# Moving the GpSimd arithmetic of a hybrid mixer to VectorE and ScalarE

## The chip, the core and the metric

The kernel runs on one core of a Trainium2 chip. A core has five engines with their own instruction streams: TensorE (PE, matrix products; PEld is its weight load), VectorE (DVE), ScalarE (ACT), GpSimd (POOL) and SyncE (SP). Here SP and POOL also issue transfers between HBM and the on-chip memory SBUF. Each engine works through its stream strictly in order and waits on semaphores that other engines raise. The metric is device time in microseconds of one launch; lower is better.

## The reference

Two layers (DEPTH 2) of a decoder trunk on 512 tokens with model width 1024, all float32. What matters here is the mixer in the middle of each layer:

```
h += 1/2 * SwiGLU_1(rmsnorm(h))                 # width 2816
u  = rmsnorm(h) @ w_in                          # one projection, split into three groups
  A: RG-LRU, width 256:  y = gelu(gate) * scan(a, sqrt(1 - a*a) * (i * x)),  a = exp(-8 * r * softplus(-lam))
                         r, i = sigmoid(block-diagonal products of conv(x))
  B: sliding-window attention, 8 query heads, window 128, a learned sink per head
  C: gated DeltaNet, 4 heads, chunks of 64:  T = (I + strict(beta k k' * decay))^-1,
                         u = T (beta v),  w = T (beta k exp(g));  a scan over 8 chunk states
                         o = rmsnorm(o) * dn_norm * silu(z)
h += concat(A, B, C) @ w_out
h += 1/2 * SwiGLU_2(rmsnorm(h))
h += sigmoid(rmsnorm(h) @ w_ple_gate) * (p[l] @ w_ple_proj)
```

A final RMSNorm follows the second layer.

## The kernel before

Every product that needs float32 accuracy is made of three passes of a reduced format: `split` and `weight` (L116 to L125) write a high half `wh` (a copy on ACT, L123) and a low half `wl` (weight minus high half, L124), and `mm3` (L147 to L149) multiplies high by high, high by low activations, and low by high. A weight block of the mixer's input projection has 128 x 1024 elements, and there are 15 of them (`proj(i)`, L912).

A layer runs FFN 1, the mixer, FFN 2 and the per-layer embedding one after the other. The two FFNs take most of the run and are not touched. The mixer of layer 0 lies at about 380 to 575 us of the profiled span, that of layer 1 some 1007 us later.

In the mixer the three groups are interwoven. `masked(t)` (L1262) writes, for each of four token tiles, the triangle times the log decay of each head (`tg`, high and low half), from which PE sums cumulative decays (R, L1274). `chunk(t)` (L1269) builds the decay matrices DT on DVE (L1290), the products of keys (`pk`, L1281) and the scaled queries and keys (L1297, L1306, L1309). The inverse of the 64 x 64 triangles starts with a chain of 15 steps on 16-row blocks that DVE alone does (L1364 to L1366: shuffle, multiply `row`, add to `x`); its result is laid out as TMA and TT (L1371, L1376), and PE then doubles the block size in `level` (L1386, `pinv`). The LRU is `lru_gates` (L957: products `pr` and `pi`, then sigmoid and two tanh on ACT, L968 on DVE), `lru_scan` (L970) and `lru_gelu` (L988). Attention computes scores `sc` (L1007), a maximum on DVE (L1011), exponentials on ACT (L1023) and scales the weights `e` of four heads by 1/dn (L140 on DVE or POOL, L134 on ACT). The chunk scan, its decay matrix `ei` (L1446) and the output product follow.

PE's order is written out by hand: ORDER and GAPS name the pieces and the amount of projection work that `fill` puts between them. The orders of DVE, ACT and POOL in the mixer come from the tile scheduler, which ranks ready instructions by its own cost estimate. The table OPT gives the engine of some operations: `es` the four heads of a scaling, `wlo` the low halves of projections 6 to 14, `g2` and `sx` one multiply each of the LRU. V is VectorE, A ScalarE, G GpSimd. POOL also issues the 86 accumulating weight transfers of the FFNs (L414) and multiplies at the end (L1646).

Of the kernel before, what the change touches and what calls it, by code (L numbers as in the profile page):

```python
# [9 lines left out]
F32 = mybir.dt.float32  # L10
# [29 lines left out]

OPT = {'pta': 'V', 'ptb': 'A', 'es': 'VAAG', 'uw': 'A', 'pn': 'A', 'bt': 'VA', 'sx': 'V', 'g2': 'G', 'wlo': 'GGVGVGVGG'}

# [20 lines left out]
def trunk(ctx: ExitStack, tc: tile.TileContext, a):  # L63
# [51 lines left out]

    def weight(src, k, n, via=None, raw=None):  # L116
        if raw is None:
            raw = wrp.tile([128, k, n], F32, tag="wr", name="wr")
            nc.sync.dma_start(out=raw, in_=src)
        hi = whp.tile([128, k, n], F32R, tag="wh", name="wh")  # L120
        lo = whp.tile([128, k, n], F32R, tag="wl", name="wl")
        with tc.high_priority():
            A.activation(out=hi, in_=raw, func=AF.Copy)  # L123
            (via or V).tensor_tensor(out=lo, in0=raw, in1=hi.bitcast(F32), op=ALU.subtract)  # L124
        return hi, lo  # L125
# [6 lines left out]
    def copy(eng, out, in_, scale=1.0):  # L132
        if eng == "A":
            A.activation(out=out, in_=in_, func=AF.Copy, scale=scale)  # L134
        else:
# [3 lines left out]
            else:  # L139
                e.tensor_scalar(out=out, in0=in_, scalar1=scale, scalar2=None, op0=ALU.mult)  # L140

    def eng(c):
        return V if c == "V" else G

# [734 lines left out]
    def mixer(l, norm, gain, ahead):  # L879
        xh, xl = norm.xh, norm.xl  # L880
        pl = par[:, l, :]
        with ExitStack() as es:
# [29 lines left out]
            def proj(i):  # L912
                wh, wl = weight(a["wi"][l, i], KD, 128, via=eng(OPT['wlo'][i - 6]) if i > 5 else None)
                ps = bank([128, S], "pp")
                for k in range(KD):
                    mm3(ps, wh[:, k, :], wl[:, k, :], xh[k], xl[k], k == 0, k == KD - 1)
                    yield 0.64
                return ps
# [51 lines left out]
            def lru_scan():  # L970
# [4 lines left out]
                for i in range(2):  # L975

                    r1, t_, x = lr[i], ltm[i], xr[i]
                    A.activation(out=r1, in_=r1, func=AF.Copy, scale=0.5, bias=0.5)
                    V.scalar_tensor_tensor(out=t_, in0=t_, scalar=1.0, in1=r1, op0=ALU.add, op1=ALU.mult)
                    V.scalar_tensor_tensor(out=r1, in0=t_, scalar=2.0, in1=r1, op0=ALU.subtract, op1=ALU.mult)  # L980
                    A.activation(out=t_, in_=r1, func=AF.Copy, scale=-2.0, bias=-1.0)
                    V.scalar_tensor_tensor(out=x, in0=r1, scalar=-1.0, in1=x, op0=ALU.mult, op1=ALU.mult)
                    eng(OPT['sx']).tensor_tensor(out=x, in0=sq[:, i, :], in1=x, op=ALU.mult)
                    V.tensor_tensor_scan(out=r1, data0=t_, data1=x, initial=0.0, op0=ALU.mult, op1=ALU.add)
                    lo_[i] = r1

            def lru_gelu(i, gl):
                g2 = pair("g2", i)  # L988
                A.activation(out=g2, in_=gl, func=AF.Square)
                A.activation(out=g2, in_=g2, func=AF.Copy, scale=0.044715, bias=1.0)  # L990
                eng(OPT['g2']).tensor_tensor(out=g2, in0=g2, in1=gl, op=ALU.mult)
                A.activation(out=g2, in_=g2, func=AF.Tanh, scale=0.7978845608028654)
# [238 lines left out]
            for t in range(NT):  # L1231
# [5 lines left out]
                z3 = zz[t].rearrange("p (h e) -> p h e", h=4)  # L1237
                G.tensor_tensor(out=z3, in0=z3, in1=dnn.unsqueeze(1).to_broadcast([128, 4, 64]), op=ALU.mult)

# [22 lines left out]
            def masked(t):  # L1262
                tg[t] = [dp.tile([128, 4, 128], F32R, tag="d", name="tg") for x in range(2)]
                for o, x in zip(tg[t], (gh, gl_)):
                    G.tensor_tensor(out=o, in0=tri.unsqueeze(1).to_broadcast([128, 4, 128]),
                                    in1=x.bitcast(F32)[:, 4 * t:4 * t + 4].unsqueeze(2).to_broadcast([128, 4, 128]),
                                    op=ALU.mult)

            def chunk(t):  # L1269
# [23 lines left out]
                for hh in range(2):  # L1293
                    rs = slice(64 * hh, 64 * hh + 64)
                    A.activation(out=er[rs].rearrange("p (c i) -> p c i", c=2), in_=R[rs, 2 * hh:2 * hh + 2, :],
                                 func=AF.Exp)
                G.tensor_tensor(out=qg[t], in0=kq[:, :, 1, tsl], in1=er.rearrange("p (c i) -> p c i", c=2),  # L1297
                                op=ALU.mult)
                for hh, pk in enumerate(pks):
# [5 lines left out]
                kv = ktm[t].rearrange("p c (h d) -> p h c d", h=2)  # L1305
                G.tensor_tensor(out=vk[t][:, :, 64:128].rearrange("p (h c) d -> p h c d", h=2), in0=kv,  # L1306
                                in1=eg[:, 4 * t:4 * t + 4].rearrange("p (h c) -> p h c", h=2).unsqueeze(3)
                                .to_broadcast([128, 2, 2, 64]), op=ALU.mult)
                G.tensor_tensor(out=kd[t].rearrange("p c (h d) -> p h c d", h=2), in0=kv,  # L1309
                                in1=cd[:, 4 * t:4 * t + 4].rearrange("p (h c) -> p h c", h=2).unsqueeze(3)  # L1310
# [49 lines left out]
            x16 = small("x16", 256).rearrange("p (u j) -> p u j", u=16)  # L1360
            G.tensor_copy(out=x16, in_=cst[:, K_D16:K_D16 + 16].unsqueeze(1).to_broadcast([128, 16, 16]))
            for i in range(15, 0, -1):
# [77 lines left out]
            def steps(t):  # L1440
# [3 lines left out]
                for hh in range(2):  # L1444
                    rs = slice(64 * hh, 64 * hh + 64)
                    G.tensor_tensor(out=ei[rs], in0=ident[rs, rs].unsqueeze(1).unsqueeze(1).to_broadcast([64, 2, 2, 64]),  # L1446
                                    in1=egl[rs, :, 4 * t + 2 * hh:4 * t + 2 * hh + 2].unsqueeze(3).to_broadcast([64, 2, 2, 64]), op=ALU.mult)
# [371 lines left out]
```

## Time and profile before

| what | value |
|---|---|
| median of 3 runs | 2054.86 us (2052.04 to 2055.87) |
| the profiled execution | 2052.92 us |
| its span, first to last instruction | 2051.1 us |
| PE busy | 1967.7 us (96%), granted clock 0.980 |
| DVE busy | 1509.4 us (74%) |
| ACT busy | 1002.0 us (49%) |
| POOL busy | 181.2 us (9%) |

Busy shares are means over the whole run. The change lies in two mixers, so the stretches of a mixer are what has to be read, and in them PE's waits and the state of DVE and ACT.

### The profile page before, as it was taken

Reading aid. Unit: us, or ns where it says so; the run is one execution under the profiler, and the core shown is the slowest. Engines: PE = TensorE matmul, PEld = TensorE weight load, DVE = VectorE, ACT = ScalarE, POOL = GpSimd, SP = SyncE. Lnnn points to the kernel's source line nnn. Section 1 sums busy time; section 2 is a strip of 40 time slices with the busy share of each in tenths; the row PEclk is TensorE's granted clock in tenths of the full one; section 3 lists DMA queues with packets and bytes.
Section 4 is the critical chain, followed back from the end, with each engine's and each line's share of the span. In section 5 each row is a group of like instructions: output and inputs, shape, how many; then the busy total and the mean of one; then the engine's idle time right before and its main releaser. Section 6 shows DMA issues by size and latency. Waiting matters only on the chain.

```text
span 2051.1 us, 32033 instructions
## 1 busy us (share of the span) xinstructions
PE 1967.7 (96%) x12625; PEld 1752.2 (85%) x12625; DVE 1509.4 (74%) x2620; ACT 1002.0 (49%) x1651; POOL 181.2 (9%) x197
## 2 busy tenths in 40 slices
PE   7999999999999999999989999999899999999996
PEld 5988998887778989997879899988677899899885
DVE  7875883879878856865888568647897887488466
ACT  5642652454745534643556336434366565156343
POOL 0100000042201000000000000000421000000001
PEclk8999999999999999999999999999999999999998
DMA  6763743221046745643457357322111377275411
GB/s 193 194 172 95 188 129 113 78 73 47 17 124 171 188 120 147 174 126 103 124 136 189 114 148 186 124 83 96 53 42 44 117 201 192 76 188 139 136 62 62
DMA packets 85415, 254.51 MB, mean 124 GB/s; under 512 B 9616, under 2 KB 17040, under 8 KB 85008
## 3 DMA queue, kind: packets, MB, share of 16 engines
q1 hardware_dynamic: 72880, 207.36, 31.8%
q0 software_dynamic: 12384, 45.09, 12.5%
q8 instruction: 99, 1.62, 0.3%
q14 instruction: 52, 0.43, 0.1%
HBM read 250.32 MB, written 2.10 MB: 123 GB/s over the span
## 4 chain that ended last, share of the span: by engine, by line
PE 75%; DVE 16%; ACT 4%; issue 3%; DMA 1%; SPq 0%; DVEq 0%; ACTq 0%
PE pu L475 10%; PE pg L475 10%; PE pd L147 8%; PE pd L149 8%; PE qu L475 8%; PE pd L148 8%; PE qg L475 7%; PE pp L147 2%; PE pp L148 1%; PE pp L149 1%; PE ppg L149 1%; PE ppg L148 1%; PE ppg L147 1%; DVE wl L124 1%; DVE gl L443 1%
## 5 line engine op out<-in xcount | busy, mean ns | idle before, releaser
L475 PE MATMUL pu<-T,gh 128*128 128x256 f32 x880 | 159.5, 280 | 0.0
L475 PE MATMUL pg<-T,gh 128*128 128x256 f32 x784 | 144.4, 282 | 9.5 <-ACT T L251 7.5
L443 DVE TENSOR_TENSOR gl<-wr,gh 128x1024 fp32r<-128x1024 f32 x102 | 124.6, 1221 | 26.6 <-ACT gh L438 26.6
L123 ACT ACTIVATE wh<-wr 128x1024 fp32r<-128x1024 f32 (+2 forms) x76 | 77.2, 1015 | 135.1 <-PE pp L148 50.5
L475 PEld LDWEIGHTS pu<-T,gh 128*128 128x128 f32 x880 | 134.7, 188 | 0.0
L129 DVE TENSOR_TENSOR gl<-wr,gh 128x1024 fp32r<-128x1024 f32 x53 | 64.5, 1223 | 93.6 <-ACT gh L128 93.4
L475 PEld LDWEIGHTS pg<-T,gh 128*128 128x128 f32 x784 | 121.2, 189 | 11.1 <-ACT T L251 8.1
L147 PE MATMUL pd<-X,gh 128*128 128x512 f32 x328 | 128.8, 393 | 0.0
L149 PE MATMUL pd<-X,gl 128*128 128x512 f32 x328 | 128.7, 392 | 0.0
L148 PE MATMUL pd<-X,gh 128*128 128x512 f32 x328 | 127.8, 390 | 0.0
L475 PE MATMUL pu<-T,gl 128*128 128x256 f32 x440 | 123.0, 279 | 0.0
L438 ACT ACTIVATE gh<-wr 128x1024 fp32r<-128x1024 f32 x102 | 105.2, 1046 | 19.9 <-PE pd L148 14.0
L128 ACT ACTIVATE gh<-wr 128x1024 fp32r<-128x1024 f32 x53 | 55.8, 1059 | 120.7 <-PE pd L148 95.2
L475 PE MATMUL pg<-T,gl 128*128 128x256 f32 x392 | 110.1, 281 | 0.0
L475 PE MATMUL pg<-T,wh 128*128 128x256 f32 x592 | 107.3, 280 | 2.3 <-DVE cg L554 2.3
L124 DVE TENSOR_TENSOR wl<-wr,wh 128x1024 fp32r<-128x1024 f32 (+2 forms) x64 | 74.1, 1157 | 40.9 <-ACT wh L123 40.2
L147 PE MATMUL pp<-X,wh 128*128 128x512 f32 x240 | 102.1, 425 | 0.0
L438 ACT ACTIVATE sh<-r 128x512 fp32r<-128x512 f32 x80 | 50.6, 632 | 103.6 <-DVE r L455 103.6
L149 PE MATMUL pp<-X,wl 128*128 128x512 f32 x240 | 98.2, 409 | 2.0 <-DVE wl L124 2.0
L443 DVE TENSOR_TENSOR wl<-wr,wh 128x1024 fp32r<-128x1024 f32 x67 | 81.8, 1221 | 23.4 <-ACT wh L438 23.4
L148 PE MATMUL pp<-X,wh 128*128 128x512 f32 x240 | 98.2, 409 | 0.2 <-DVE X L252 0.2
L475 PEld LDWEIGHTS pg<-T,wh 128*128 128x128 f32 x592 | 90.5, 188 | 3.2 <-DVE cg L554 2.9
(477 smaller groups left out, 6048.9 us busy)
## 6 DMA issues: line engine op xcount, KB each, us to landing
wr<-in_d_dram SPq DMA_DIRECT2D x64, 512.0 KB, 3.9
wr<-in_g_dram SPq DMA_DIRECT2D x45, 512.0 KB, 4.3
wr<-in_u_dram SPq DMA_DIRECT2D x45, 512.0 KB, 4.3
r<-in_g_dram SPq DMA_DIRECT2D x43, 512.0 KB, 3.7
r<-in_u_dram SPq DMA_DIRECT2D x43, 512.0 KB, 4.1
r<-in_g_dram POOLq DMA_DIRECT2D x43, 512.0 KB, 7.3
r<-in_u_dram POOLq DMA_DIRECT2D x43, 512.0 KB, 6.9
wr<-in_wi_dram SPq DMA_DIRECT2D x30, 512.0 KB, 3.3
```

Source lines behind the costliest of these rows:

```text
L123: A.activation(out=hi, in_=raw, func=AF.Copy)
L124: (via or V).tensor_tensor(out=lo, in0=raw, in1=hi.bitcast(F32), op=ALU.subtract)
L128: A.activation(out=hi, in_=x, func=AF.Copy)
L129: V.tensor_tensor(out=lo, in0=x, in1=hi.bitcast(F32), op=ALU.subtract)
L147: T.matmul(out=out, lhsT=wh, rhs=xh, start=start, stop=False)
L148: T.matmul(out=out, lhsT=wh, rhs=xl, start=False, stop=False)
L149: T.matmul(out=out, lhsT=wl, rhs=xh, start=False, stop=stop)
L438: A.activation(out=self.g[n][0], in_=self.of(n)[0], func=AF.Copy)
L443: V.tensor_tensor(out=g[1], in0=raw, in1=g[0].bitcast(F32), op=ALU.subtract)
L475: T.matmul(out=ps, lhsT=l_[:, q, :], rhs=r_, start=start and q == 0 and i == 0, stop=stop and q == 3 and i == 2, skip_group_check=more)
```

## The change

All tensor operations of the mixer that POOL did move. Per layer, DVE takes six low halves of projection weights (wlo), L1238 (4 instructions), L1297, L1306 and L1309 (4 each), L1446 (8 of 64 x 256) and L991 (2); ACT takes `masked` (8 instructions of 128 x 512 become 32 of 128 x 128, one per head, because ACT scales by one number per partition), the fourth head of each attention scaling (8) and the constant copy into x16 (1). POOL keeps L414 and L1646. Lines of the new kernel from L142 on have numbers lower by 3, from L1265 on by 4.

```diff
-OPT = {'pta': 'V', 'ptb': 'A', 'es': 'VAAG', 'uw': 'A', 'pn': 'A', 'bt': 'VA', 'sx': 'V', 'g2': 'G', 'wlo': 'GGVGVGVGG'}
+OPT = {'pta': 'V', 'ptb': 'A', 'es': 'VAAA', 'uw': 'A', 'pn': 'A', 'bt': 'VA'}
...
-    def weight(src, k, n, via=None, raw=None):
+    def weight(src, k, n, raw=None):
...
-            (via or V).tensor_tensor(out=lo, in0=raw, in1=hi.bitcast(F32), op=ALU.subtract)
+            V.tensor_tensor(out=lo, in0=raw, in1=hi.bitcast(F32), op=ALU.subtract)
...
-                wh, wl = weight(a["wi"][l, i], KD, 128, via=eng(OPT['wlo'][i - 6]) if i > 5 else None)
+                wh, wl = weight(a["wi"][l, i], KD, 128)
...
-                eng(OPT['g2']).tensor_tensor(out=g2, in0=g2, in1=gl, op=ALU.mult)
+                V.tensor_tensor(out=g2, in0=g2, in1=gl, op=ALU.mult)
...
-                G.tensor_tensor(out=z3, in0=z3, in1=dnn.unsqueeze(1).to_broadcast([128, 4, 64]), op=ALU.mult)
+                V.tensor_tensor(out=z3, in0=z3, in1=dnn.unsqueeze(1).to_broadcast([128, 4, 64]), op=ALU.mult)
...
-                    G.tensor_tensor(out=o, in0=tri.unsqueeze(1).to_broadcast([128, 4, 128]),
-                                    in1=x.bitcast(F32)[:, 4 * t:4 * t + 4].unsqueeze(2).to_broadcast([128, 4, 128]),
-                                    op=ALU.mult)
+                    for h in range(4):
+                        A.activation(out=o[:, h, :], in_=tri, func=AF.Copy, scale=x.bitcast(F32)[:, 4 * t + h:4 * t + h + 1])
...
-                G.tensor_tensor(out=qg[t], in0=kq[:, :, 1, tsl], in1=er.rearrange("p (c i) -> p c i", c=2),
+                V.tensor_tensor(out=qg[t], in0=kq[:, :, 1, tsl], in1=er.rearrange("p (c i) -> p c i", c=2),
...
-            G.tensor_copy(out=x16, in_=cst[:, K_D16:K_D16 + 16].unsqueeze(1).to_broadcast([128, 16, 16]))
+            A.activation(func=AF.Copy, out=x16, in_=cst[:, K_D16:K_D16 + 16].unsqueeze(1).to_broadcast([128, 16, 16]))
...
-                    G.tensor_tensor(out=ei[rs], in0=ident[rs, rs].unsqueeze(1).unsqueeze(1).to_broadcast([64, 2, 2, 64]),
+                    V.tensor_tensor(out=ei[rs], in0=ident[rs, rs].unsqueeze(1).unsqueeze(1).to_broadcast([64, 2, 2, 64]),
```

The two instructions of L1306 and L1309 change from G to V in the same way. PE's and SP's orders stay as they were. The orders of DVE and ACT in the mixer come out anew.

First place: DVE in layer 0 where the first projection behind the chunks needs its low half. LTA and DT belong to the chunks, `l` is the input of the 16-row chain. Before:

```order
L1300 TENSOR_TENSOR LTA<-pk,DT 128x256 x2
L1063 SCALAR_TENSOR_TENSOR T_4550<-pp,rb 128x512
L1302 TENSOR_TENSOR DT<-pk,DT 128x256 x2
L1354 STREAM_TRANSPOSE l_4751<-LTA 32x512 x3
L124 TENSOR_TENSOR wl<-wr,wh 128x1024
L1354 STREAM_TRANSPOSE l_4751<-LTA 32x512
L1343 TENSOR_TENSOR vk<-pv,vr 128x4x64 x2
L1357 TENSOR_SCALAR er<-l_4751,cst 128x256
```

After:

```order
L1296 TENSOR_TENSOR LTA<-pk,DT 128x256 x3
L1060 SCALAR_TENSOR_TENSOR T_4574<-pp,rb 128x512
L1296 TENSOR_TENSOR LTA<-pk,DT 128x256
L124 TENSOR_TENSOR wl<-wr,wh 128x1024
L1298 TENSOR_TENSOR DT<-pk,DT 128x256 x4
L1350 STREAM_TRANSPOSE l_4775<-LTA 32x512 x4
```

The low half (L124) stood behind three of the four transposes (L1354, now L1350) and now stands ahead of all of them, and two of the chunk's own products come behind it.

Second place: ACT in layer 0 behind the LRU's gate products (`pr`, `pi` the products, T the sigmoids, `tm` and `sq` the two tanh; a table load stands where the function set changes). Before:

```order
L965 ACT_TABLE_LOAD
L965 ACTIVATE T_4708<-pr,par 128x512
L966 ACTIVATE sq<-pi,nb 128x512
L967 ACTIVATE tm<-T_4708,lrr 128x512
L965 ACTIVATE T_4719<-pr,par 128x512
L974 ACT_TABLE_LOAD
L974 ACTIVATE T_4708<-T_4708,lsp_4287 128x512
L966 ACTIVATE sq<-pi,nb 128x512
L967 ACTIVATE tm<-T_4719,lrr 128x512
L978 ACTIVATE T_4708<-T_4708 128x512
L974 ACTIVATE T_4719<-T_4719,lsp_4287 128x512
L978 ACTIVATE T_4719<-T_4719 128x512
```

After:

```order
L962 ACT_TABLE_LOAD
L962 ACTIVATE T_4732<-pr,par 128x512
L964 ACTIVATE tm<-T_4732,lrr 128x512
L963 ACTIVATE sq<-pi,nb 128x512
L971 ACT_TABLE_LOAD
L971 ACTIVATE T_4732<-T_4732,lsp_4287 128x512
L962 ACT_TABLE_LOAD
L962 ACTIVATE T_4743<-pr,par 128x512
L963 ACTIVATE sq<-pi,nb 128x512
L975 ACTIVATE T_4732<-T_4732 128x512
L964 ACTIVATE tm<-T_4743,lrr 128x512
L969 ACT_TABLE_LOAD
```

The first sigmoid is now followed by an exponential before the second sigmoid, which puts two more table loads into the sequence, and the second `sq` comes behind both.

Third place: DVE in layer 1 where the inverse's 16-row chain (`row`, `x`) ends and TMA is laid out. Before, around TMA:

```order
L1365 TENSOR_TENSOR row<-row,x_14848 128x16
L1366 TENSOR_TENSOR x_14848<-x_14848,row 128x16
L1371 TENSOR_TENSOR TMA<-x_14848,cst 128x512 x2
L968 SCALAR_TENSOR_TENSOR T_14788<-sq,T_14788 128x512
L1371 TENSOR_TENSOR TMA<-x_14848,cst 128x512 x2
L1376 STREAM_TRANSPOSE TT<-TMA 128x512 x4
L979 SCALAR_TENSOR_TENSOR tm<-tm,T_14797 128x512
L979 SCALAR_TENSOR_TENSOR tm<-tm,T_14808 128x512
L1058 TENSOR_TENSOR T_14958<-pp,rb 128x512
L980 SCALAR_TENSOR_TENSOR T_14797<-tm,T_14797 128x512
L980 SCALAR_TENSOR_TENSOR T_14808<-tm,T_14808 128x512
L982 SCALAR_TENSOR_TENSOR T_14641<-T_14797,T_14641 128x512
```

After, ahead of TMA:

```order
L977 SCALAR_TENSOR_TENSOR T_14845<-tm,T_14845 128x512
L1362 TENSOR_TENSOR x_14896<-x_14896,row 128x16x2
L977 SCALAR_TENSOR_TENSOR T_14856<-tm,T_14856 128x512
L979 SCALAR_TENSOR_TENSOR T_14689<-T_14845,T_14689 128x512
L1361 TENSOR_TENSOR row<-row,x_14896 128x16
L1442 TENSOR_TENSOR row<-cst,egl 64x256 x2
L979 SCALAR_TENSOR_TENSOR T_14836<-T_14856,T_14836 128x512
L980 TENSOR_TENSOR T_14689<-sq,T_14689 128x512
L1362 TENSOR_TENSOR x_14896<-x_14896,row 128x16
L980 TENSOR_TENSOR T_14836<-sq,T_14836 128x512
L981 SCALAR_TENSOR_TENSOR T_14845<-tm,T_14689 128x512
L1367 TENSOR_TENSOR TMA<-x_14896,cst 128x512 x4
```

The LRU's chain of both halves up to the first scan (before: L979, L980, L982, L983, L984; now L976, L977, L979, L980, L981) stood behind TMA and TT and now stands ahead of TMA, with two of the L1446 (now L1442) among it.

## Rows read from the trace of the kernel before

**Rows 1.** POOL's groups of instructions over the whole run: busy us, mean ns; then idle before.
```profile
L124 POOL TENSOR_TENSOR wl<-wr,wh 128x1024 fp32r<-128x1024 f32 x12 | 29.3, 2443 | 146.0 <-ACT wh L123 138.3 <-PE pr L961 7.7
L140 POOL TENSOR_SCALAR e<-e,dn 128x256 f32<-128x256 f32 x12 | 11.6, 965 | 48.1 <-DVE dn L1026 33.1 <-ACT X L128 8.4 <-ACT T L134 6.7
L1446 POOL TENSOR_TENSOR row<-cst,egl 64x256 f32<-64x256 f32 x16 | 11.3, 706 | 8.7 <-DVE x L1366 4.8 <-DVE LTA L1462 3.3
L1265 POOL TENSOR_TENSOR tg<-cst,gh 128x512 fp32r<-128x512 f32 x8 | 8.3, 1040 | 6.3 <-ACT gh L128 6.3
```

**Rows 2.** Stretches of layer 0's mixer: length, each engine's busy us, granted clock, DMA share, GB/s.
```profile
440.00:480.00 40.00, 32.60 (x152) 24.03 (x151) 37.50 (x76) 14.94 (x36) 18.52 (x19) 0.94 0.17 56
...
490.00:530.00 40.00, 38.16 (x230) 32.14 (x228) 38.63 (x83) 27.29 (x48) 11.42 (x9) 0.96 0.13 44
530.00:570.00 40.00, 39.30 (x326) 27.67 (x324) 31.84 (x137) 29.00 (x97) 8.23 (x10) 1.00 0.00 1
```

**Rows 3.** PE's waits between 440 and 580 us: total us, times, longest us.
```profile
PE sc L1007 <- DVE mx L1011: 3.7, 3, 1.7
PE pk L1281 <- DVE xs L922: 3.0, 1, 3.0
PE sc L1007 <- DVE T L1099: 1.6, 1, 1.6
PE pp L149 <- DVE wl L124: 1.0, 1, 1.0
```

**Rows 4.** POOL in order of time, two of the mixer's weight halves: start, us.
```profile
453.21 2.40 POOL L124 TENSOR_TENSOR wl<-wr,wh 128x1024 fp32r<-128x1024 f32 x1
...
476.16 2.35 POOL L124 TENSOR_TENSOR wl<-wr,wh 128x1024 fp32r<-128x1024 f32 x1 [12.86 <-ACT wh L123]
```

**Rows 5.** DVE in order of time in the same stretch: start us, us taken, count at the end.
```profile
450.67 5.08 DVE L1290 SCALAR_TENSOR_TENSOR DT<-DT,b,cst 128x128 f32<-128x128 f32 x4
...
460.09 1.70 DVE L1290 SCALAR_TENSOR_TENSOR DT<-DT,b,cst 128x128 f32<-128x128 f32 x4 [0.18 <-ACT DT L1287]
...
468.57 1.23 DVE L124 TENSOR_TENSOR wl<-wr,wh 128x1024 fp32r<-128x1024 f32 x1
...
475.13 0.39 DVE L1365 TENSOR_TENSOR row<-row,x 128x224 f32<-128x224 f32 x1
...
476.63 2.11 DVE L1365 TENSOR_TENSOR row<-row,x 128x208 f32<-128x208 f32 x1
```

**Rows 6.** ACT in order of time: four small scaled copies, two per-head scalings.
```profile
443.92 1.14 ACT L1285 ACTIVATE DT<-R,gc 128x128 f32<-128x128 f32 x4
...
533.39 0.90 ACT L134 ACTIVATE e<-e,dn 128x256 f32<-128x256 f32 x2
```

**Rows 7.** Two stretches in which the granted clock was half.
```profile
478.80:485.40 6.60, 5.84 (x16) 4.56 (x17) 6.53 (x41) 2.17 (x11) 0.33 (x1) 0.51 0.18 60
523.20:526.40 3.20, 3.20 (x16) 2.79 (x14) 3.17 (x15) 2.30 (x9) 1.27 (x1) 0.52 0.36 127
```

**Rows 8.** PE in layer 1's mixer, the gate product and the inverse's first level.
```profile
1495.93 1.02 PE L961 MATMUL pr<-T,lw 128*128 128x512 f32 x2
...
1504.19 1.95 PE L1386 MATMUL pinv<-TMA,LTA 128*128 128x128 f32 x16
```

**Rows 9.** ACT in layer 1's mixer behind the gate products.
```profile
1505.11 0.63 ACT L978 ACTIVATE T<-T 128x512 f32<-128x512 f32 x1
1505.76 1.28 ACT L972 ACT_TABLE_LOAD   x1
1507.05 1.06 ACT L972 ACTIVATE sq<-tm 128x1024 f32<-128x1024 f32 x1
```

**Rows 10.** DVE in layer 1's mixer.
```profile
1502.64 2.16 DVE L1371 TENSOR_TENSOR TMA<-x,cst 128x512 f32<-128x512 f32 x2
...
1509.37 1.25 DVE L979 SCALAR_TENSOR_TENSOR tm<-tm,T 128x512 f32<-128x512 f32 x2
...
1517.59 3.15 DVE L984 TENSOR_TENSOR_SCAN T<-tm,T 128x512 f32<-128x512 f32 x2
```

More of the change, by code (lines that the diff above doesn't have):

```diff
@@ L140, in copy @@
                 e.tensor_scalar(out=out, in0=in_, scalar1=scale, scalar2=None, op0=ALU.mult)
-    def eng(c):
-        return V if c == "V" else G
     def mm3(out, wh, wl, xh, xl, start, stop):
@@ L982, in lru_scan @@
                     V.scalar_tensor_tensor(out=x, in0=r1, scalar=-1.0, in1=x, op0=ALU.mult, op1=ALU.mult)
-                    eng(OPT['sx']).tensor_tensor(out=x, in0=sq[:, i, :], in1=x, op=ALU.mult)
+                    V.tensor_tensor(out=x, in0=sq[:, i, :], in1=x, op=ALU.mult)
                     V.tensor_tensor_scan(out=r1, data0=t_, data1=x, initial=0.0, op0=ALU.mult, op1=ALU.add)
@@ L1305, in chunk @@
                 kv = ktm[t].rearrange("p c (h d) -> p h c d", h=2)
-                G.tensor_tensor(out=vk[t][:, :, 64:128].rearrange("p (h c) d -> p h c d", h=2), in0=kv,
+                V.tensor_tensor(out=vk[t][:, :, 64:128].rearrange("p (h c) d -> p h c d", h=2), in0=kv,
                                 in1=eg[:, 4 * t:4 * t + 4].rearrange("p (h c) -> p h c", h=2).unsqueeze(3)
                                 .to_broadcast([128, 2, 2, 64]), op=ALU.mult)
-                G.tensor_tensor(out=kd[t].rearrange("p c (h d) -> p h c d", h=2), in0=kv,
+                V.tensor_tensor(out=kd[t].rearrange("p c (h d) -> p h c d", h=2), in0=kv,
                                 in1=cd[:, 4 * t:4 * t + 4].rearrange("p (h c) -> p h c", h=2).unsqueeze(3)
```

## The prediction

> **What bounds the kernel now.** Read the stretches of a mixer first, then PE's waits in it, then DVE and POOL side by side, and only then the order of instructions. From 440 to 480 us DVE is busy 37.50 of 40 us while PE is busy 32.60, and from 490 to 530 DVE is at 38.63 with PE at 38.16; from 530 to 570 PE is at 39.30, and ACT is the fuller of the other two around its softmax work, with 29.00 [rows 2]. So in the first 40 us DVE sets the pace, after that PE does with DVE close behind. PE's waits say the same: all four large ones in this mixer end on DVE, 3.0 us for the key products on `xs`, 1.0 on a low half, 1.6 on T of L1099 and 3.7 in three pieces on the attention's maximum [rows 3]. They come to 9.3 us per mixer. Layer 1's mixer has the same pattern; I use layer 0's numbers for both.
>
> Part of DVE's load is not its own. Four products of L1290 took 1.70 us at 460.09, and the same four took 5.08 at 450.67, over a POOL low half that began at 453.21 and took 2.40. A `row` multiply of 208 columns took 2.11 us at 476.63, where the larger one with 224 columns just before took 0.39; POOL's low half ran from 476.16 to 478.51 and the multiply ended at 478.74 [rows 4, 5]. Both have two inputs in SBUF, and both end when POOL ends, plus their own work. The Trainium skill (SBUF — State Buffer, "SBUF: two separate sides") says that DVE and GpSimd hold one shared pair of ports as an exclusive lock for a whole instruction, also for a DVE operation with two SBUF inputs against a GpSimd operation that reads SBUF. The trace agrees: had the two shared evenly, 0.39 us would have become about 0.8, not 2.11.
>
> How much of this DVE pays per mixer lies between the 5.1 us of the two cases (3.4 and 1.7) and POOL's busy time in the three stretches, 18.52 + 11.42 + 8.23 = 38.2 us [rows 2]. I take 19, half of the upper end, since about half of what runs on DVE in these stretches has two SBUF inputs.
>
> **The change part by part.** *DVE's account.* Six low halves at 1.23 us [rows 5] are 7.4 us in place of 2.44 each on POOL [rows 1]. Sixteen instructions of 128 x 256 at 0.39, the time of the row multiply of about that size, are 6.2. Eight of 64 x 256 cost at most as much, I take 0.3: 2.4. Two of 128 x 512 at 0.62, half of the 1.25 of L979 [rows 10], are 1.2. Together 17.2 us more per mixer, against 19 less of stalls: a gain of about 2, within what I know of the 19 no gain at all. What moves the time is therefore where DVE is late, not how much it does.
>
> *The early part of a mixer.* The wait of 3.0 us on `xs` goes with the stall of 3.4 in L1290 ahead of it. Next late is the exponential `er` on ACT, which the reuse of the key products' bank needs: `masked` puts 32 copies of about 0.28 us, a quarter of 1.14 [rows 6], into ACT's queue, 9.0 us where POOL took 8 x 1.04 = 8.3 [rows 1], and some of them stand in front of `er`. I leave 1.4 of the wait: -1.6, between 0 and -3.0. The 1.0 on the low half goes, since it now stands ahead of the transposes: -1.0, at worst 0. The 1.6 on L1099 shrinks by what DVE has won by then, less the low half of 1.23 that now lies there: -0.7. Of the three waits on the maximum, the one right behind the locked multiply loses that multiply's 1.7, and gets the 1.23 of a low half: -0.5. Together -3.8 per layer, between 0 and -7.3 (3.0, 1.0, 1.6 and 1.7).
>
> *The clock.* Behind such waits the granted clock was half: 0.51 from 478.8 to 485.4, 0.52 from 523.2 to 526.4 [rows 7]. At the full level of 2.4 GHz the first stretch would have been 3.3 us shorter, the second 1.6. With shorter waits ahead I take half of each back, -1.7 and -0.8, per layer, between nothing and all.
>
> *ACT's order in layer 0.* Two more table loads at 1.28 [rows 9] stand between the gate products and the second `sq`, on which the DVE instruction ahead of TMA waits (L965 of the new kernel, L968 of the old). Counted from the first gate product, the second `sq` is ready after about 8.5 us, and that instruction and the first TMA, 0.6 each, make 9.8; PE comes to the inverse 1504.19 - 1495.93 = 8.3 us after the same product [rows 8], and layer 0 has the same distance. That is a wait of about 1.6; between 0 and 2.6 (both loads). I take +1.8 with the handover. DVE has its LRU work behind it earlier than before, and the wait of 1.7 on the maximum near 520 us goes: -1.7.
>
> *DVE's order in layer 1.* This is the large one. TMA now stands behind the whole LRU chain of both halves and the first scan, and the chain needs the second L978 on ACT. In ACT's new order that one is behind the table load and the square root. Before, it started at 1505.11; with 1.28 and 1.06 ahead of it and 0.63 of its own it ends at about 1508.0 [rows 9]. Then DVE has seven instructions of 128 x 512 at 0.62 (4.4), two of L1446 (0.6), three small steps of the 16-row chain at about 0.2 (0.6), one scan at 3.15 / 2 = 1.6, and the first TMA at 0.6: 7.8 us [rows 10], so TMA is there at 1515.8. PE comes to it at 1504.19 [rows 8]. Nothing hides that, for PE's order is fixed and every projection, score and output product is queued behind this product. PE waits 11.5 us; I see 10 as the lower end (less for each small step) and 13 as the upper one (two of the instructions took 1.4 each under POOL's stalls before). Behind it, -1.7 for the wait near 520 as in layer 0, and a stretch at half clock: by [rows 7] between 1.6 and 3.3, I take +2.5.
>
> *The tail.* The fourth head of each scaling on ACT costs 0.90 / 2 = 0.45 where POOL took 0.97 [rows 1, 6], eight times, in the stretch where ACT is at 29.00 of 40 [rows 2] and at nine tenths around its exponentials. Between 0 (PE runs at 39.30, all hidden) and 3.6; I take +1.0 per layer. The copy into x16 and L1238 lie where DVE and ACT have room: nothing. SP's order is the same, and the POOL transfers of FFN 2 wait for a tile that ACT writes, not for POOL's multiplies: nothing earlier there.
>
> *Sum.* Layer 0: -3.8 -1.7 +1.8 -1.7 -0.8 +1.0 = -5.2. Layer 1: -3.8 -1.7 +11.5 -1.7 -0.8 +2.5 +1.0 = +7.0. Together +1.8 on the profiled execution of 2052.92, so 2054.7. The median of the runs shown is 1.94 higher, 2054.86; on it the forecast is 2056.7, which is no change: 0.2%, 4.1 us here, is about what a measurement can tell.
>
> The Trainium skill has a rule against this change (Perfetto Trace Analysis, "Optimizing Scalar/DVE Operations"): where DVE is saturated, giving work to GpSimd may make sense, though it adds that the shared port may undo it. By the first half the time would be that of the third rival, by the second half that of the sum.
>
> **The rivals.** *The lock was worth more (faster).* The early waits go whole (-7.3 in place of -3.8 per layer) and both slow stretches too (-4.9 in place of -2.5): 11.8 less than the sum, about 2045. For it: every one of these waits ends on DVE, and a stall in front of a wait counts in full. Against it: low halves of 1.23 us lie in front of the same waits now, and ACT's 32 copies. Half of it, 2050.8, is the edge to faster. A layer 1 wait of 6 instead of 11.5 would do the same, but I see nothing that shortens it so far.
>
> *ACT and DVE take the place of POOL (slower).* The 32 copies stand in front of `er` and of the copies of the high halves, so that PE's key products and projections wait for ACT as they did for DVE. Then the early gain and the clock's fall to half: 2.75 of 5.5 per layer, 5.5 more, 2062; from a loss of 1.2 us per layer on it is slower by more than 4.1 - 1.8 = 2.3. For it: ACT was busy 14.94 of 40 us there [rows 2], and 9.0 are added at one end of that stretch. Against it: that is still room for it all, if the order is right.
>
> *The stalls are not POOL's (slower).* Then DVE has 17.2 us more per mixer, with 2.5 and 1.4 us free in two stretches of 40 [rows 2], and PE waits for most of the 13 that are left in each: up to 26, and about 2071 if half of it is hidden.
>
> **How the numbers follow.** Forecast 0.42, with its own range 2051 to 2060 from layer 1's wait (-1.5, +1.5), layer 0's (-1.8, +0.8) and the tail; lock worth more 0.25; ACT and DVE in POOL's place 0.26; stalls not POOL's 0.07. The range 2046 to 2066 holds the forecast, nearly all of the second and most of the third case. The forecast's range lies above 2050.8 and just reaches over 2059.0, so that faster has 0.26, within 0.2% has 0.40, slower has 0.34.
>
> **What would show it.** Right: no DVE instruction in the mixers above three times its usual time; PE's wait on the low half gone and that on `xs` under 2 us or turned to ACT; one wait of 10 to 13 us of PE on TMA in layer 1 and one of about 2 in layer 0; layer 0's mixer 3 to 7 us shorter, layer 1's 5 to 9 longer. Wrong: no such wait in layer 1, stalls of the same size on DVE with POOL idle, or PE waiting on `er`, `tg` or high halves for more than 3 us per mixer.

## The result: slower by 0.57%

The changed kernel takes 2065.71 us (median of 4 runs, 2062.58 to 2069.73) against 2054.48 of the kernel before in the same comparison; the ratio is 1.0057, with a 95% interval of 1.0036 to 1.0078. The forecast was no change, 2056.7, with its own range of 2051 to 2060; the time lies beyond that and at the upper end of the wide range, 2046 to 2066, and the kernel moved where it was forecast to stand still.

**The profile after.** The profiled execution took 2069.73 us, the longest of the four, with a span of 2068.0. POOL's tensor work is gone, and DVE's busy time over the run fell although it got more instructions:

```profile
PE 1974.2 (95%) x12625; PEld 1757.1 (85%) x12625; DVE 1504.7 (73%) x2684; ACT 1030.3 (50%) x1734; POOL 81.1 (4%) x99
```

The three stretches of layer 0's mixer that answer to [rows 2], in the same columns:

```profile
440.00:480.00 40.00, 37.02 (x173) 27.79 (x171) 36.31 (x102) 23.04 (x65) 0.00 (x0) 0.96 0.19 63
490.00:530.00 40.00, 35.20 (x223) 29.09 (x222) 35.00 (x81) 27.68 (x57) 0.00 (x0) 0.96 0.10 34
530.00:570.00 40.00, 38.34 (x311) 26.71 (x311) 31.03 (x131) 27.66 (x90) 0.00 (x0) 1.00 0.00 1
```

In the first, PE has 4.4 us more of its work behind it with DVE no fuller than before. The second has turned round: PE 3.0 us less, with DVE at 35.00 where it had 38.63. So PE waits more, though DVE is less busy. The same times hold somewhat later work than before (the gate products begin at 482.5 us, where they began at 488.6), so what the change cost is read from the stages below.

The products of L1290 (now L1286) and the row multiply of 208 columns, which answer to [rows 5]: four products in 1.13 where they took 5.08 and 1.70, and the multiply in 0.37 where it took 2.11.

```profile
450.28 1.13 DVE L1286 SCALAR_TENSOR_TENSOR DT<-DT,b,cst 128x128 f32<-128x128 f32 x4
...
478.32 0.37 DVE L1361 TENSOR_TENSOR row<-row,x 128x208 f32<-128x208 f32 x1
```

PE's waits in layer 0's mixer, which answer to [rows 3]:

```profile
PE pinv L1382 <- DVE TMA L1367: 2.4, 1, 2.4
PE ptr L1035 <- DVE e L140: 1.9, 1, 1.9
PE ptr L1035 <- ACT e L134: 1.8, 3, 0.8
PE pk L1277 <- ACT er L1291: 1.3, 1, 1.3
PE sc L1004 <- DVE mx L1008: 1.2, 2, 0.9
PE sc L1004 <- DVE T L1096: 0.8, 1, 0.8
```

and in layer 1's, the first rows of the same view from 1440 to 1600 us:

```profile
PE pinv L1382 <- DVE TMA L1367: 11.2, 1, 11.2
PE sc L1004 <- DVE T L1096: 2.1, 1, 2.1
```

In layer 0 the four waits of before are smaller or gone; in layer 1 the one on T of L1099 (now L1096) grew from 1.6 to 2.1. New are the one for TMA, 2.4 and 11.2 us, and those for the softmax weights `e` in front of their transposes, which came to 0.4 us before.

Where the time went, by stages of PE's work (its order is the same in both, so each stage runs from the start of its first product to that of the next). The second column is the kernel before in another execution, from the first experiment below; outside the mixers is counted from PE's first product to its last:

| stage, us | before | before, repeated | after |
|---|---|---|---|
| layer 0: projections, chunks, first scores | 115.7 | 114.2 | 106.7 |
| gate products up to the inverse | 8.3 | 8.3 | 10.8 |
| inverse up to the chunk scan | 50.9 | 50.9 | 54.3 |
| layer 1: projections, chunks, first scores | 114.3 | 113.3 | 107.8 |
| gate products up to the inverse | 8.3 | 8.3 | 19.6 |
| inverse up to the chunk scan | 50.9 | 50.0 | 55.2 |
| chunk scan and output product, both layers | 144.5 | 144.5 | 144.5 |
| everything outside the mixers | 1549.6 | 1552.6 | 1560.2 |

The two mixers together are 5.9 us longer than in the first profile of before and 9.3 longer than in the second.

### The profile page after: what moved, and what is told of

Read it like the earlier page. It is cut to its first block, busy times and chain, and to the rows that moved or that the text cites. A ratio compares the mean times of both kernels' runs of the same rounds, so it can differ in the third digit from the quotient of the medians.

```text
span 2068.0 us, 32005 instructions
## 1 busy us (share of the span) xinstructions
PE 1974.2 (95%) x12625; PEld 1757.1 (85%) x12625; DVE 1504.7 (73%) x2684; ACT 1030.3 (50%) x1734; POOL 81.1 (4%) x99
## 4 chain that ended last, share of the span: by engine, by line
PE 76%; DVE 14%; ACT 6%; issue 2%; DMA 1%; SPq 0%; DVEq 0%; ACTq 0%
PE pu L472 10%; PE pg L472 10%; PE qu L472 8%; PE pd L144 8%; PE pd L146 8%; PE pd L145 8%; PE qg L472 7%; PE pp L144 2%; PE pp L145 2%; PE pp L146 2%; DVE wl L124 1%; PE ppg L146 1%; DMA wr<-in_d_dram 1%; PE ppg L145 1%; PE ppg L144 1%
## 5 line engine op out<-in xcount | busy, mean ns | idle before, releaser
L472 PE MATMUL pg<-T,gh 128*128 128x256 f32 x784 | 144.5, 282 | 9.4 <-ACT T L248 7.4
L472 PEld LDWEIGHTS pg<-T,gh 128*128 128x128 f32 x784 | 121.3, 189 | 10.9 <-ACT T L248 8.0
L124 DVE TENSOR_TENSOR wl<-wr,wh 128x1024 fp32r<-128x1024 f32 (+2 forms) x76 | 88.7, 1168 | 49.6 <-ACT wh L123 49.4
```

Source lines behind the costliest of these rows:

```text
L124: V.tensor_tensor(out=lo, in0=raw, in1=hi.bitcast(F32), op=ALU.subtract)
L472: T.matmul(out=ps, lhsT=l_[:, q, :], rhs=r_, start=start and q == 0 and i == 0, stop=stop and q == 3 and i == 2, skip_group_check=more)
```

## The experiments

Each is compared with the kernel before on the same chip; the median of before is 2053.95 to 2054.75 us in all of them, so their times can be set side by side. Where the text says "stage", it is one of the table; the "late stage" is the one from the inverse up to the chunk scan, and the "chunks' stage" is the part of the first row from the first `pk` to the first scores (34.5 and 35.1 us before).

**e1, the kernel before once more.** No edit.

> The kernel before once more, nothing changed, to see how far its profiled execution moves. If the 10.6 us by which the FFN stages of the new kernel's profiled execution are longer (2.9, 2.1, 1.5, 2.5 and 1.6 us in five stages whose instructions did not change) are a matter of the execution and not of the change, this repeat's FFN stages differ from those of the first profile by about as much, some of them by over 1 us, while the mixers agree within 1 us. If they come from the change, the repeat's FFN stages agree with the first profile within 0.5 us each. The ratio to before is 1.000 within 0.002 by both.

2052.84 us, ratio 0.9990 (0.9981 to 1.0000). The mixers agreed less well than expected: layer 0's projections were 3.2 us shorter and its chunks 1.6 longer. Outside the mixers the first FFN was 3.5 longer, the part around FFN 1 of layer 1 2.3 shorter, the end 1.8 longer. A stage of one execution is known to some 2 or 3 us where PE has long waits or slow stretches in it, and the 10.6 us outside the mixers in the profiled execution after are such a difference. The code there is the same in all fourteen profiled executions of this case: the first profile of before is the shortest of them, 1549.6, the one after the change the longest, 1560.2, and the twelve others lie between 1550 and 1558, with a mean of 1555 for the kernels made from the one before and the same for those made from the changed one.

**e2, TMA ahead of the LRU.** The change as it is; the 16-row chain and TMA are emitted ahead of the last projection work in front of them, and the LRU's DVE work takes its constant 1.0 from an element written after TMA was read.

```diff
+            late = x16[:, 0, 0:1]
+            V.tensor_scalar(out=late, in0=late, scalar1=0.0, scalar2=1.0, op0=ALU.mult, op1=ALU.add)
...
-                V.scalar_tensor_tensor(out=xr[i], in0=ti, scalar=1.0, in1=xr[i], op0=ALU.add, op1=ALU.mult)
+                V.scalar_tensor_tensor(out=xr[i], in0=ti, scalar=late, in1=xr[i], op0=ALU.add, op1=ALU.mult)
...
-                    V.scalar_tensor_tensor(out=t_, in0=t_, scalar=1.0, in1=r1, op0=ALU.add, op1=ALU.mult)
+                    V.scalar_tensor_tensor(out=t_, in0=t_, scalar=late, in1=r1, op0=ALU.add, op1=ALU.mult)
```

> The changed kernel with the LRU's DVE work held behind TMA by a dependency in both layers (one instruction of one column more per layer), the rest as it is. Theory: the waits of PE for TMA (2.4 us in layer 0, 11.2 in layer 1) come from the order of DVE alone; both go to under 0.5 us, and with the slower clock behind them (2.1 us in layer 1) the kernel gains 11 to 16 us, to about 2052 on the median of 2065.7; if what follows gives some back, as the softmax part did in the new kernel (5 to 6 us per layer), 2056 to 2060. Rival: DVE has too much to do for TMA to be in time whatever the order; then at least 5 us of the wait in layer 1 stays, and the time is above 2060.

2054.22 us, ratio 0.9998 (0.9986 to 1.0009): the 11 us are back, within the band expected. The wait for TMA is gone from the lists of both layers; that of layer 1, which began with 11.2 us in the changed kernel, now begins:

```profile
PE ptr L1035 <- DVE e L140: 2.5, 1, 2.5
PE sc L1004 <- DVE T L1096: 2.1, 1, 2.1
PE sc L1004 <- DVE mx L1008: 1.4, 3, 0.9
```

So the order of DVE at this one place, and not its load, is worth as much as the whole difference between the kernels. The gate stages are 8.2 and 8.6 us; the stage behind them is still 56.4 and 54.9.

**e3, only the low halves to DVE.** The kernel before with one letter changed six times.

```diff
-OPT = {... 'wlo': 'GGVGVGVGG'}
+OPT = {... 'wlo': 'VVVVVVVVV'}
```

> The kernel before with only the six low halves of projection weights per layer moved from POOL to DVE (12 instructions of 1.23 us). Theory of the lock: DVE instructions with two SBUF inputs stall while a POOL instruction reads SBUF; the stalled row multiplies (2.1 and 2.3 us) come down to 0.4 or less, the four products of L1290 lose about 2.4 of their 5.1 us, PE's wait of 1.0 on a low half goes or stays under 1, and DVE's busy time in 440 to 530 us rises by less than 3 us though it has 7.4 us more work; the kernel gains 0 to 6 us. Rival, the stalls are not POOL's: they stay, DVE's busy time rises by 7 us per mixer, and the kernel loses 4 to 12 us.

2047.22 us, ratio 0.9952 (0.9938 to 0.9966): faster than the kernel before. The slowest row multiply is 0.60 us (before: 2.28). From 440 to 530 us DVE is less busy than before, first row before and second row e3, though it has more to do:

```profile
440.00:530.00 90.00, 80.76 (x409) 63.53 (x407) 82.94 (x197) 46.09 (x96) 30.79 (x29) 0.92 0.14 47
```

```profile
440.00:530.00 90.00, 81.45 (x431) 63.99 (x431) 81.66 (x211) 52.40 (x109) 21.74 (x26) 0.94 0.15 47
```

The gain, 7.5 us, is more than the 0 to 6 expected; the table's first stage is 6.0 and 3.5 us shorter than before, and layer 1's late stage 3.5. The wait of PE on a low half did not shrink as expected, it grew to 3.7 us; the gain came in spite of it.

**e4, only the fourth softmax head to ACT.**

```diff
-OPT = {... 'es': 'VAAG', ...}
+OPT = {... 'es': 'VAAA', ...}
```

> The kernel before with only the fourth head of each attention scaling moved from POOL to ACT (16 instructions of 0.45 us instead of 0.97). Between the last level of the inverse and the chunk scan the changed kernel lost 5 to 6 us per layer (waits of PE for e before the transposes). Theory 1, the added scaling on ACT is that loss: this kernel loses it too, 8 to 12 us in all. Theory 2, the softmax chain was the pace there anyway and only gives back what PE had won before it: this kernel changes by under 2 us. As predicted, 1.0 per layer: 2 us slower.

2055.59 us, ratio 1.0003 (0.9989 to 1.0017), and the late stage is 50.7 and 50.1 us. In this order the added scaling by itself costs nothing that can be measured; theory 1 and the predicted 1.0 per layer fall.

**e5, e2 with the gelu multiply back on POOL.**

```diff
-                V.tensor_tensor(out=g2, in0=g2, in1=gl, op=ALU.mult)
+                G.tensor_tensor(out=g2, in0=g2, in1=gl, op=ALU.mult)
```

> The kernel of e2_tma_first with the LRU's gelu multiply (L991 of the kernel before, two instructions per layer) back on POOL, nothing else. e4 left the loss between the inverse and the chunk scan unexplained (3.3 and 4.3 us longer than before in the new kernel, 5.5 and 4.0 in e2). Theory: on DVE that multiply and its successors stand between the attention's maximum and the negated maximum that ACT's exponentials need, so the exponentials start about 1.7 us late and PE waits for the scaled weights; back on POOL the negated maximum stands right behind the maximum again, the two waits near 520 and 530 us (2.2 and 1.3 in layer 0, 2.5 in layer 1) go for the most part, and the stage is 2 to 4 us shorter per layer: 4 to 8 us off the 2054.2 of e2, 2046 to 2050. Rival: the stage only gives back what PE had won ahead of it, with the softmax chain as its pace; then the stage stays within 1 us and the time at 2054.

2054.41 us, ratio 0.9994 (0.9981 to 1.0008). The late stage fell to 53.7 in layer 0 and rose to 56.0 in layer 1. In layer 0 PE's waits for `e` fell to 0.5 us as expected, but a new one of 3.0 on ACT's copy `pn` came; in layer 1 they stayed, 2.6 and 2.3. Neither theory holds: the one instruction helps in one layer and not in the other.

**e6, e2 with gelu multiply, L1446 and the fourth head back on POOL.**

```diff
-                V.tensor_tensor(out=g2, in0=g2, in1=gl, op=ALU.mult)
+                G.tensor_tensor(out=g2, in0=g2, in1=gl, op=ALU.mult)
...
-                    V.tensor_tensor(out=ei[rs], ...
+                    G.tensor_tensor(out=ei[rs], ...
...
-                    copy(OPT['es'][h], ...
+                    copy('VAAG'[h], ...
```

> The kernel of e2_tma_first with the gelu multiply, the chunk scan's decay matrices (L1446) and the fourth head of the scalings (L140) all back on POOL: everything behind the inverse as before the change, everything ahead of it as after. Theory: the late loss is one of DVE's order by these instructions; the stage from the inverse to the chunk scan comes back to 51 us or less in both layers, and the kernel takes 2054.2 less 9.5, about 2044 to 2047, which is faster than both. If e5 has all of the gain, this one equals it within 2 us. Rival as in e5: 2054.

2047.72 us, ratio 0.9967 (0.9952 to 0.9982): faster than before, though not by all that was expected. Layer 0's late stage is 50.0, layer 1's 55.9. In layer 1 ACT still does the second group's exponentials (128 x 256) ahead of the first group's scaling (128 x 128), for which PE waits:

```profile
1528.27 0.49 ACT L1020 ACTIVATE e<-e,nm 128x256 f32<-128x256 f32 x1
...
1528.76 1.50 ACT L134 ACTIVATE e<-e,dn 128x128 f32<-128x128 f32 x4
```

**e7, the lock by itself.** e3, with POOL repeating the six subtractions into a tile that nothing reads (`again` is set for the six projections of e3).

```diff
             V.tensor_tensor(out=lo, in0=raw, in1=hi.bitcast(F32), op=ALU.subtract)
+            if again:
+                G.tensor_tensor(out=raw, in0=raw, in1=hi.bitcast(F32), op=ALU.subtract)
```

> The kernel of e3_low_halves_only, and POOL does the same six subtractions per layer once more, into the raw weight tile that nothing reads any more, behind DVE's own. DVE's work is that of e3, POOL's that of before. Theory of the lock: DVE instructions with two inputs in SBUF stall again (some single ones above 1.5 us; the sixteen L1290 above e3's 610 ns on average), DVE's busy time in 440 to 530 us is 5 us or more above that of e3, and the kernel loses 4 to 15 us on e3 (2047.2), to 2051 or more. Rival, POOL's instructions do not stall DVE and e3 was faster for another reason: DVE's durations as in e3, time within 3 us of it.

2060.11 us, ratio 1.0033 (1.0020 to 1.0046), 12.9 us above e3. DVE's busy time from 440 to 530 us is 85.78, 4.1 above e3 and not 5. The sixteen L1290 are hardly slower than in e3, 636 ns against 610; the stalls fell on other instructions. One of POOL's repeats, and the LRU's multiplies under it on DVE (L984 here is L982 of before, 1.28 us for the same two in e3):

```profile
508.01 2.69 POOL L126 TENSOR_TENSOR wr<-wr,wh 128x1024 f32<-128x1024 f32 x1 [9.01 <-issue]
```

```profile
507.80 3.45 DVE L984 SCALAR_TENSOR_TENSOR T<-T,T 128x512 f32<-128x512 f32 x2
511.17 0.73 DVE L1396 COPY_PREDICATED TMA<-cst,pinv 128x512 f32<-128x512 uint32 x1
```

The pair ends at 511.25, behind POOL's end at 510.70. The repeats also keep the raw tile longer and come ahead of `tg` on POOL (PE waits 1.3 us for it), so not all of the 12.9 is the lock. That DVE stalls under POOL and not otherwise is shown: of the DVE instructions of the two mixers up to the chunk scan that last over 0.5 us, 30 take more than twice the shortest of their line and shape here, 20 in e3, 26 before, and none after the change or in e2, where POOL has none of the mixers' work.

**e8, only the masked decays to ACT.** The edit is that of L1265 in the change.

> The kernel before with only the masked decays moved from POOL to ACT (32 copies of 128 x 128 per layer in place of 8 of 128 x 512). Read in the stage of the chunks, which the whole change made 3.8 and 4.8 us shorter and e3 did not (0.6 longer, 2.0 shorter): theory 1, the locks of the eight masked instructions were the other part of DVE's stalls there, then the stage is 2 to 5 us shorter here too and L1290's sixteen fall from 747 ns to 600 or less on average; theory 2, ACT's 9.0 us delay the exponential that PE waits for, then the stage is no shorter or longer. In layer 0 DVE's order now has part of the LRU's chain ahead of TMA (not in layer 1), so PE is expected to wait 4 to 8 us for TMA there, which says again that the scheduler's order and not the work decides this wait.

2057.12 us, ratio 1.0010 (0.9997 to 1.0022). The sixteen L1290 fell to 551 ns each, but the chunks' stage is 33.3 and 35.2 us, 1.2 shorter and the same: in between the two theories. PE waits 6.9 us for TMA in layer 0, as expected, and 2.9 in layer 1, where none was expected. A change that touches no instruction of that chain moved it there as well.

**e9 and e10, scaling ahead of the next exponentials.** One buffer for the denominators in place of two, in e2 (e9) and in e6 (e10).

```diff
-                dn = small("dn", 4, bufs=2)
+                dn = small("dn", 4)
```

> The kernel of e2_tma_first with one buffer instead of two for the softmax denominators (dn), so that ACT cannot begin the next group's exponentials before a group's weights are scaled; all moved work stays on VectorE and ScalarE. e5 and e6 showed the late loss to differ by layer: in the traces ACT's order puts the four exponentials of the second group (4 x 0.49 us) ahead of the scaling of the first in layer 1 of e6 and in layer 0 of the new kernel. Theory: that order is the larger part of the late loss; PE's waits for e of L140 and L134 in front of the transposes (1.3 and 1.2 us in layer 0 of e2, 2.5 and 1.2 in layer 1) fall to half or less, and the stage from the inverse to the chunk scan, 56.4 and 54.9 us in e2, comes to 52 to 54 in both, the kernel to 2047 to 2051. Rival: the denominators' single buffer delays as much as it mends, or the lateness comes from DVE (the negated maximum behind two other instructions) alone; then the stage stays within 1 us of e2's and the time at 2054.

> e6_tail_back with the same single buffer for dn: low halves, chunk products and masked decays off POOL, the work behind the inverse on POOL as before, TMA ahead of the LRU, scaling ahead of the next exponentials. Theory: layer 1's stage from the inverse to the chunk scan, 55.9 us in e6, comes to 50 to 52 as layer 0's did, and the kernel takes 4 to 6 us less than e6's 2047.7: 2041 to 2044, faster than both kernels. Rival: layer 1's loss is DVE's order (the negated maximum behind a predicated copy and a gelu step, 1.3 us), then at most 1 to 2 us are gained: 2046.

e9: 2049.34 us, ratio 0.9982 (0.9971 to 0.9994); the late stage is 55.2 and 52.1, so 1.2 and 2.8 less: in layer 1 as expected, in layer 0 1.2 above the band. The time is within its band, but PE's waits for `e` of L140, 2.1 and 2.5 us, did not fall. e10: 2042.69 us, ratio 0.9956 (0.9942 to 0.9971), faster than both kernels and as expected; late stages 50.0 and 53.3, in layer 1 above the 50 to 52 expected. Its stretches, against those after the change:

```profile
440.00:480.00 40.00, 35.74 (x167) 26.84 (x166) 36.57 (x102) 23.40 (x65) 0.00 (x0) 0.96 0.20 63
490.00:530.00 40.00, 38.22 (x256) 31.94 (x254) 36.30 (x85) 30.35 (x61) 6.06 (x6) 1.00 0.11 34
530.00:570.00 40.00, 39.35 (x321) 27.96 (x321) 32.02 (x131) 25.79 (x87) 8.15 (x10) 1.00 0.07 23
```

PE is back at 38.22 from 490 to 530 us, and the granted clock does not fall there.

**e11 and e12, the negated maximum on ACT,** in e9 (e11) and e10 (e12).

```diff
-                V.tensor_scalar(out=nm, in0=mx, scalar1=-1.0, scalar2=None, op0=ALU.mult)
+                A.activation(out=nm, in_=mx, func=AF.Copy, scale=-1.0)
```

> e9_scaling_first with the negated maximum computed on ACT in place of DVE, so that it follows the maximum directly and not behind a predicated copy and a gelu step; all the work that the change moved stays on VectorE and ScalarE. Theory: what is left of the late loss is that lateness of 1.2 to 1.9 us; PE's wait for e of L140 (2.1 and 2.5 us in e9) falls under 1, the stage from the inverse to the chunk scan goes from 55.2 and 52.1 to about 53 and 50.5, and the kernel to 2044 to 2047. Rival: DVE is full there with the moved gelu multiply and matrices, so the maximum itself comes late; the stage stays within 1 us of e9's and the time at 2049.

> e10_best with the negated maximum on ACT. Theory: layer 1's stage from the inverse to the chunk scan goes from 53.3 to 51 or less with PE's wait of 2.0 us for e of L140 under 1; layer 0's, with no such wait, stays at 50; the kernel gains 1 to 3 us on 2042.7. Rival as for e11: no change, 2042 to 2043.5.

e11: 2047.71 us, ratio 0.9976 (0.9965 to 0.9988), its late stages 55.2 and 53.6, no shorter; e12: 2042.77 us, ratio 0.9951 (0.9936 to 0.9966), late stages 50.2 and 53.1. No stage became shorter, as the rivals said; that DVE is full there, the reason e11's rival gives, is not shown by it. In e12 the denominators, not the maximum, stand late in layer 1:

```profile
1520.00 0.14 DVE L1022 TENSOR_TENSOR dn<-dn,es 128x4 f32<-128x4 f32 x1
...
1520.14 0.71 DVE L1399 COPY_PREDICATED TT<-cst,pinv 128x512 f32<-128x512 uint32 x1
1520.75 0.67 DVE L129 TENSOR_TENSOR X<-T,X 128x512 fp32r<-128x512 f32 x1
1521.35 0.17 DVE L1023 RECIPROCAL dn<-dn 128x4 f32<-128x4 f32 x1
```

That these 1.2 us between sum and reciprocal are what PE still waits for in layer 1 (1.8 us for `e` of L140) is argued and was not tried.

## Why the prediction was wrong

**The lock: right.** Under POOL's work DVE stalls, without it not (e7). L1290's sixteen in layer 0, 551 ns in e8, stand as follows before, in e3 and after:

```profile
L1290 DVE SCALAR_TENSOR_TENSOR DT<-DT,b,cst 128x128 f32<-128x128 f32 x16 | 11.1, 747 | 0.2 <-ACT DT L1287 0.2
```

```profile
L1290 DVE SCALAR_TENSOR_TENSOR DT<-DT,b,cst 128x128 f32<-128x128 f32 x16 | 8.9, 610 | 0.0
```

```profile
L1286 DVE SCALAR_TENSOR_TENSOR DT<-DT,b,cst 128x128 f32<-128x128 f32 x16 | 4.5, 348 | 0.0
```

DVE's account came out a little better than the gain of 2 us per mixer: its busy time over the run fell by 4.7.

**The early part: right, and larger than forecast.** -5.5 per layer with the clock; measured -9.0 and -6.5 against the first profile, -7.5 and -5.5 against the repeat. As predicted, the wait on `xs` turned into one on `er` of ACT, 1.3 us against the 1.4 left. ACT's 32 copies took 10.5 us per layer, not 9.0, without more harm than that.

**The two orders around TMA: right in place and size.** +1.8 predicted and +2.5 measured in layer 0; 11.5 predicted and 11.3 measured in layer 1. In layer 0, where the first gate product starts at 482.5 us, DVE waits for the second `sq` of ACT in front of TMA:

```profile
491.23 0.68 ACT L963 ACTIVATE sq<-pi,nb 128x512 f32<-128x512 f32 x1
```

```profile
491.94 0.69 DVE L965 SCALAR_TENSOR_TENSOR T<-sq,T 128x512 f32<-128x512 f32 x1 [1.66 <-ACT sq L963]
492.55 2.49 DVE L1367 TENSOR_TENSOR TMA<-x,cst 128x512 f32<-128x512 f32 x4
```

In layer 1, the rows that answer to [rows 9] and [rows 10]: the second L978 (now L975) ends at 1504.89 behind load and square root, which is 12.0 us after the first gate product (1492.86) where 12.1 was forecast (1508.0 less 1495.93), and DVE then works through the chain to TMA.

```profile
1502.02 1.28 ACT L969 ACT_TABLE_LOAD   x1
1503.32 1.06 ACT L969 ACTIVATE sq<-tm 128x1024 f32<-128x1024 f32 x1
1504.28 0.61 ACT L975 ACTIVATE T<-T 128x512 f32<-128x512 f32 x1
```

```profile
1505.21 0.68 DVE L976 SCALAR_TENSOR_TENSOR tm<-tm,T 128x512 f32<-128x512 f32 x1
...
1510.59 1.22 DVE L981 TENSOR_TENSOR_SCAN T<-tm,T 128x512 f32<-128x512 f32 x1
1511.73 2.47 DVE L1367 TENSOR_TENSOR TMA<-x,cst 128x512 f32<-128x512 f32 x4
```

At the end of this wait and behind it, from 1508 to 1518, the granted clock was 0.57, and PE lost 2.1 us in its next products where +2.5 was forecast. The wait of 1.7 near 520 us went, as forecast: by the second scores behind it PE had won 3.8 us in each layer, where 2.5 was the term. The slow stretch that followed that wait did not go, it came later (below).

**The tail: the step that failed.** The prediction took "+1.0 per layer" for it, as the price of the fourth head on ACT, and put the order of the softmax at nothing. Measured, PE lost 6.9 us in layer 0 and 6.0 in layer 1 between those scores and the chunk scan, 10.9 more than the term in all. The operation that I priced was innocent in the order of the kernel before (e4); alone in the new order it was not tried. What I left out is that DVE's and ACT's orders of the softmax were made anew as well. Before, in layer 0, ACT scales the first group ahead of the second group's exponentials:

```profile
528.84 0.69 ACT L134 ACTIVATE e<-e,dn 128x128 f32<-128x128 f32 x2 [0.54 <-DVE dn L1026]
530.36 0.51 ACT L1023 ACTIVATE e<-e,nm 128x256 f32<-128x256 f32 x1 [0.83 <-DVE nm L1017]
```

After the change it does the second group's exponentials, 523.84 to 525.82, and only then the first group's scaling:

```profile
525.33 0.49 ACT L1020 ACTIVATE e<-e,nm 128x256 f32<-128x256 f32 x1
...
525.82 0.97 ACT L134 ACTIVATE e<-e,dn 128x128 f32<-128x128 f32 x3
```

and PE, which is early by then, waits at the transposes for DVE's head and then for ACT's:

```profile
525.39 0.33 PE L1035 MATMUL ptr<-cst,e 128*128 128x128 f32 x1 [1.89 <-DVE e L140]
526.26 1.06 PE L1035 MATMUL ptr<-cst,e 128*128 128x128 f32 x3 [0.54 <-ACT e L134]
```

In all PE waits 3.7 us for `e` in layer 0, and behind the first of these waits the granted clock was 0.71 from 525.4 to 531.2 us (0.74 from 1545.0 to 1551.5 in layer 1): the slow stretch of which the term -0.8 gave half back had only moved. Part of this was also there to be read in [rows 2]: from 530 to 570 us DVE, with 31.84, is fuller than ACT, with 29.00, and not the other way round as the prediction has it, and the first of the new waits is one on DVE.

I had compared the orders at the LRU and at TMA, where the diff puts its instructions, and not where the same scheduler lays out work that the diff does not name. Of the 4 to 6 us by which this stage is above 50, e9 shows 1.2 and 2.8 to be the order on ACT; e6 shows that in layer 0 the rest goes with the three operations of the stage put back on POOL, which changes DVE's and ACT's load there together with their order, so that the two are not told apart; in layer 1 some 3 us stay open.

**The sum.** With the terms as measured the mixers come to 5.9 to 9.3 us more where 1.8 was forecast, the medians to 11.2 (7.4 to 16.0). Against the first profile the late stage missed by 8.2 us in all (-1.5 and +1.0 forecast, +3.4 and +4.3 measured), and it was luck that the early part, 4.5 better than forecast, hid half of that. The remainder is not found outside the mixers, where the kernels made from either one agree (e1); 9.3 is inside the interval and 5.9 just short of it.

**The rivals.** "ACT and DVE take the place of POOL" had the sign and nearly the size, and the wrong mechanism: the early gain did come. In the late stages, which became longer, DVE is busy for a smaller share of the time than before (47.0 of 54.3 us in layer 0 and 42.0 of 55.2 in layer 1, before 45.9 of 50.9 and 45.8 of 50.9). "The lock was worth more" fits the kernel in which the order is held: e10 is 11 us faster than before, with most of the change in it and three operations back on POOL. The 2071 of the third rival does not follow from its own terms; 2056.7 and 13 give 2070.

## What to carry to other kernels

Where a scheduler decides the order, a change of engines is two changes: its work and the new order, here -13 to -16 us in the early part against +21 to +22 behind it. Compare the orders over the whole stretch that is scheduled anew, at each place where the bounding engine waits, and not only around the moved instructions. If a stage gets slower with its engines less busy, look at the order first: hold it by a dependency (a constant written late, one buffer in place of two) before the change is judged.

## What was not expected of the hardware

The same wait of PE in the same FFN code was followed by the full clock in one execution and by half of it in another. In layer 0's FFN 2, behind a wait of 2.01 us before and 1.96 after, these three us follow (first before, then after), with 25 and 14 products done:

```profile
653.20:656.20 3.00, 3.00 (x25) 3.00 (x26) 3.00 (x5) 2.20 (x3) 0.00 (x0) 1.00 0.85 283
```

```profile
653.00:656.00 3.00, 3.00 (x14) 3.00 (x15) 2.11 (x4) 1.57 (x3) 0.00 (x0) 0.50 0.85 274
```

In the repeat of the kernel before the clock fell near there too (0.77 from 656 to 662 us), so it is not the change's. For the same products PE was busy 1497.3 us outside the mixers before, 1502.5 in the repeat and 1505.8 after: most of the 10.6 us is PE taking longer over them, as it does in such stretches. A difference of that size in one profile is no finding.
